# Latent attention in source order on four engines, key-tile maxima over two banks, block sums made by accumulating transfers

## The chip, the core and the metric

The kernel runs on one core of one Trainium2 chip. The metric is the time of one execution in microseconds (us). The engines are TensorE (PE, its weight loads listed apart as PEld), VectorE (DVE), ScalarE (ACT), GpSimd (POOL) and SyncE (SP), which only issues transfers here; 16 DMA engines move data between HBM and the core's memories, SBUF and PSUM. PSUM consists of banks of 512 32-bit values per partition.

## The reference

One encoder layer over 2304 tokens: a sequence of 2048 (the prompt) and one of 256 (the sample), which share weights but don't attend to each other. D_MODEL is 1024, all in 32-bit floats.

```python
h = rms_norm(x, g_mix_pre);  z = h @ w_in            # 1024 -> 256 + 128 + 32 + 3*512
c_q, c_kv, k_rope, nq, nk, nv = split(z)             # the first three are the "latents"
a = mla_attention(...)   # q = rms(c_q) @ w_q_up, k,v = rms(c_kv) @ w_kv_up, 8 heads,
                         # 96-wide keys, dense softmax(q k^T * scale) v, 64-wide values
n = neighborhood_attention(nq, nk, nv, na_rpb)       # 8 heads, window of 8 rows x 16 columns
x = x + rms_norm(concat([a, n]) @ w_o, g_mix_post)
h = rms_norm(x, g_ffn_pre)
hc = conv3(h @ w_ffn_up)                             # 1024 -> 5632, width-3 depthwise over tokens
g, u = split(hc)
x = x + rms_norm((gelu(g) * u) @ w_ffn_down, g_ffn_post)
```

## The kernel before

**Precision.** A factor is split into two rounded parts, "hi" and "lo": `split` (L93 to L96) is an ACT cast that writes hi (L95) and a DVE subtraction that writes lo (L96). A product of two split factors is three matmuls, hi·hi, lo·hi and hi·lo, which accumulate in one PSUM bank (`mm3`, L118 to L122).

**Stages in order**, with their stretch of the profile: input projection (0 to about 250 us), neighbourhood attention (250 to 695), preparation of the latent attention (695 to 793), latent attention (793 to 1657), output projection (1657 to 1910), FFN up (1910 to 2945), FFN down (2945 to 3497).

**Neighbourhood attention** runs 144 half-unit steps. Beside its own work a step carries a piece of other projections: up to step `mid` = 72 the queries and keys not yet projected (`queries_rest`), with weights in tiles `w2`; then the latent projection (`latents`, L480, 72 pieces, from step mid + 6 by `LATE`). At step mid the eight k-rows of the latents' weights are loaded and split in one burst through the `qk_hl` buffers.

**Latent attention** (`mla`, L539). For each head there are five units: four of 512 prompt queries against 16 key tiles of 128, one of 256 sample queries against 2 key tiles; 66 steps a head, 528 in all. A step's `scores` (L614) is three matmuls into `pS` (L619 to L621; three buffers), an exponential by ACT rounded to `ph` (L623), the same exponential unrounded in place (L624), DVE's difference `pl` (L626), and POOL's running sum `acc` (L634). Four steps later `values` (L638) adds two matmuls to the accumulators `po` and `pl` (L646, L647). At a unit's end `acc` is split and summed over keys, ACT and DVE take the accumulators out (`evacuate`, `add`) and `finish` (L670) transposes the result through a bank of `pm`, from which DVE takes a reciprocal and a quotient (L677, L679).

Each unit needs preparation while the one before it runs: `load` (L586) transposes its queries through `pm` and splits them from there, 16 `guard` tasks (L596; 2 for the sample) compute a hi·hi product of 128 queries with 512 keys into `pg` (L600) and its maximum (L602), and `peak` and `row` (L604, L608) turn the maxima into a row that is transposed through `pm` and appended to the queries, so that the exponential can't overflow. In heads 0 to 6 `k_chunk` (L561) also projects the next head's keys, 512 tokens at a time, three matmuls into `pm` (L120 to L122) and a split from there (`kbh`, `kbl`). `pm` has one buffer, shared by `load`, `row`, `k_chunk` and `finish`. `pg` has two.

The order of instructions on each engine in this stage comes from the framework's scheduler, which sorts by priorities and modelled durations; the source only says at which step a task is created (`spread`, `prepare`, L722 to L741). When the last head begins, `load_wo` (L898) loads and splits the eight 1024-wide rows of w_o one after the other.

**Output projection** (`out_proj`, L913): 18 token tiles, each transposed (L948), split, multiplied by w_o (48 matmuls), normed. In the first tiles `weight_sums` (L125) also loads blocks of w_ffn_up (48 loads), lets POOL form five sums or differences for six of the 22 column groups (L149) and stores them to the scratch `ws_d` in HBM. At tile 8 the FFN's pools open and its first loads start (`ffn_open`).

**FFN up** (`ffn`, L1183) is a Strassen-like scheme: for each of 3 token parts and 22 column groups j ("units", 66 of them) seven products m of 12 matmuls each (L1291), of a weight factor (a block of w_ffn_up or a sum of two blocks, `WRAW` and `WSUM`) and an x factor. In part 0, for j from 6 on, POOL forms the sums (`w_source`, L1122, five a unit, L1132) and stores them to `ws_d`; parts 1 and 2 load them. Each unit's products are combined with adds on DVE and POOL (L1194) from PSUM and from copies that ACT makes (L1231), then convolved, gated and stored.

Of the kernel before, what the change touches and what calls it, by code (L numbers as in the profile page):

```python
# [10 lines left out]
F32 = mybir.dt.float32  # L11
# [6 lines left out]
P = 128  # L18
# [28 lines left out]
class Layer:  # L47


    def __init__(self, ctx, tc, a):  # L50
# [17 lines left out]
        self.ws_d = scratch("ws_d", (NFF, 5, P, 512))  # L68
# [56 lines left out]
    def weight_sums(self, raw_buf, out_buf, todo):  # L125

        nc, a = self.nc, self.a
        raws, outs, stores = [], [], []
        todo = list(todo)

        def load():
            if todo:
                j, c = todo.pop(0)
                raw = [raw_buf().rearrange("p (a b) -> p a b", a=2) for _ in range(2)]
                for r in range(2):
                    for hf in range(2):
                        src = a["w_ffn_up"][j + r * NFF][:, 4 * hf + 2 * c:4 * hf + 2 * c + 2, :]
                        nc.sync.dma_start(out=raw[r][:, hf].rearrange("p (a b) -> p a b", b=P), in_=src)
                raws.append((j, c, raw))

        def sums():
            if outs:
                j, c, out = outs.pop(0)
                nc.sync.dma_start(out=self.ws_d[j].rearrange("n p k -> p n k")[:, :, c * 256:(c + 1) * 256], in_=out)
            if raws and (len(raws) > 1 or not todo):
                j, c, raw = raws.pop(0)
                out = out_buf().rearrange("p (n b) -> p n b", b=256)
                for m, ((r0, c0), (r1, c1), sign) in enumerate(self.WSUM.values()):
                    nc.gpsimd.tensor_tensor(out=out[:, m], in0=raw[r0][:, c0], in1=raw[r1][:, c1],  # L149
                                            op=ALU.add if sign > 0 else ALU.subtract)  # L150
                outs.append((j, c, out))

        def step():
            load()
            sums()

        def flush():
            while raws or outs:
                sums()

        return step, flush

    def front(self):
# [5 lines left out]
        with ExitStack() as s:  # L169
# [8 lines left out]

            def load_w(buf, W, c0, n, at=0):
                for k in range(KD):  # L180
                    raw = buf()
                    nc.sync.dma_start(out=raw[:, :n], in_=a["w_in"][k * P:(k + 1) * P, c0:c0 + n])
                    self.split(raw[:, :n], W[0][:, k, at:at + n], W[1][:, k, at:at + n])

            def qk_products(W, f, pq, ks, xh, xl):

                fc = slice(f * P, (f + 1) * P)
                for k in ks:
                    self.mm3(pq, W[0][:, k, fc], W[1][:, k, fc], xh[:, k, :], xl[:, k, :], k == 0, k == KD - 1)

# [37 lines left out]
            w2 = w_tiles(w2p, 3, 512)  # L228


            with ExitStack() as s1:
# [10 lines left out]
                W = [w_tiles(wp, i, n) for i, n in enumerate((512, 256, 256))]  # L242
                raw_buf = lambda: rawp.tile([P, 512], F32, name="raw")
# [35 lines left out]
                def queries(b, side):  # L279
                    xh, xl = blocks[b]  # L280
                    for f in range(4):
# [3 lines left out]
                        qk_products(W[1 + f // 2], f % 2, pq, range(KD), xh, xl)  # L285
# [9 lines left out]
                load_w(raw_buf, W[0], LAT + 1024, 512)  # L295
                n0[1]()
                load_w(raw_buf, W[1], LAT, 256)
# [3 lines left out]
                load_w(raw_buf, W[2], LAT + 512, 256)  # L301
                for b in range(nb):
# [6 lines left out]
                    if b in (2, 3):  # L309
                        load_w(raw_buf, w2, LAT + 512 * (b - 2) + 256, 256, 256 * (b - 2))  # L310
# [10 lines left out]
            sp = en(name="na_s", bufs=2)  # L321
            sm = en(name="na_sm", bufs=6)
# [145 lines left out]
            def queries_rest():  # L468
# [7 lines left out]
                qk_products(w2, f, Rest.pq, range(4 * half, 4 * half + 4), *Rest.blocks[b])  # L476
# [3 lines left out]
            def latents():  # L480
# [8 lines left out]
                for k in range(2 * part, 2 * part + 2):  # L489
                    self.mm3(Rest.pq, xh[:, k, off:off + P], xl[:, k, off:off + P], wlat[0][:, k, :], wlat[1][:, k, :],  # L490
                             k == 0, k == KD - 1)
# [4 lines left out]

            grids = [(0, 32, 4 * u) for u in range(8)] + [(SP, 4, 0)]
# [4 lines left out]
            LATE = 6  # L502
# [4 lines left out]
            for i in range(n + 6):  # L507
# [16 lines left out]
                if i + lead < mid:  # L524
                    queries_rest()
                if i == mid:
                    wlat = [w[:, :, :LAT] for w in w_tiles(w2p, 3, 512)]
                    Rest.n, Rest.blocks = 0, {0: fetch(0)}
                    load_w(lambda: st.tile([P, 2, NB], F32, name="qk_hl").rearrange("p a b -> p (a b)"), wlat, 0, LAT)
                if i >= mid + LATE and Rest.n < 4 * NT:  # L530
                    latents()
# [7 lines left out]
    def mla(self):  # L539
        nc, tc, a = self.nc, self.tc, self.a  # L540
        with ExitStack() as s:
# [15 lines left out]
            ps_g = en(name="ml_pg", bufs=2, space=PSUM)  # L557
# [11 lines left out]
            class Unit:  # L569


                def __init__(u, h, t0, nq, kt0, nkt):
                    u.h, u.t0, u.nq, u.kt0, u.nkt = h, t0, nq, kt0, nkt
                    u.nt = nq // P
                    u.nch = (nkt * P + 511) // 512
# [10 lines left out]
                def load(u):  # L586
# [7 lines left out]
                    u.mx = sm.tile([P, 4, 4], F32, name="mx")  # L594

                def guard(u, i, c):  # L596
                    n = min(512, u.nkt * P - c * 512)
                    pg = ps_g.tile([P, 512], F32, name="pg")
                    k0 = u.kt0 * P + c * 512
                    nc.tensor.matmul(out=pg[:, :n], lhsT=u.qh[0:QKD, i * P:(i + 1) * P],  # L600
# [884 lines left out]
```

## Time and profile before

| | us |
|---|---|
| median of 3 runs | 3509.79 (3509.08 to 3511.76) |
| the profiled execution | 3507.15 |
| its span | 3505.4 |
| PE busy in it | 3368.9 (96%) |
| DVE busy | 2385.9 (68%) |
| ACT busy | 1837.8 (52%) |
| POOL busy | 1376.2 (39%) |

The span is the traced part of the profiled execution; 1.75 us lie around it. A busy share says how full an engine was on average; where time is lost is read from stretches in which PE was not full, since PE carries most of the work in every stage. "PEclk" in the rows is the clock that TensorE was granted, as a share of full speed.

### The profile page before, as it was taken

Reading aid. Unit: us, or ns where it says so; the run is one execution under the profiler, and the core shown is the slowest. Engines: PE = TensorE matmul, PEld = TensorE weight load, DVE = VectorE, ACT = ScalarE, POOL = GpSimd, SP = SyncE. Lnnn points to the kernel's source line nnn. Section 1 sums busy time; section 2 is a strip of 40 time slices with the busy share of each in tenths; the row PEclk is TensorE's granted clock in tenths of the full one; section 3 lists DMA queues with packets and bytes.
Section 4 is the critical chain, followed back from the end, with each engine's and each line's share of the span. In section 5 each row is a group of like instructions: output and inputs, shape, how many; then the busy total and the mean of one; then the engine's idle time right before and its main releaser. Section 6 shows DMA issues by size and latency. Waiting matters only on the chain.

```text
span 3505.4 us, 51290 instructions
## 1 busy us (share of the span) xinstructions
PE 3368.9 (96%) x17806; PEld 2913.6 (83%) x17806; DVE 2385.9 (68%) x3774; ACT 1837.8 (52%) x3463; POOL 1376.2 (39%) x1216
## 2 busy tenths in 40 slices
PE   8999989989999999999989999899999999999999
PEld 7889979967777777766778999899989999888887
DVE  5325555588988888898345999987789776224332
ACT  4225556567777777777234544555555554223121
POOL 0022323157777778775521477632232222000110
PEclk9999999999999999999999999999999999999999
DMA  8789889341000000011995655465546555434553
GB/s 269 253 258 231 213 191 237 122 149 26 13 15 14 16 14 13 18 47 48 267 256 150 195 170 172 144 192 149 149 113 194 151 150 179 149 117 134 187 186 125
DMA packets 338068, 497.24 MB, mean 142 GB/s; under 512 B 69584, under 2 KB 213072, under 8 KB 330832
## 3 DMA queue, kind: packets, MB, share of 16 engines
q1 hardware_dynamic: 302576, 417.87, 39.7%
q0 software_dynamic: 35232, 76.10, 8.6%
q8 instruction: 140, 2.29, 0.3%
q14 instruction: 120, 0.98, 0.1%
HBM read 337.90 MB, written 155.37 MB: 141 GB/s over the span
## 4 chain that ended last, share of the span: by engine, by line
PE 74%; DVE 10%; ACT 6%; DMA 5%; issue 3%; POOL 2%; SPq 1%; ACTq 0%; POOLq 0%; DVEq 0%
PE pz L1291 21%; PE po L122 6%; PE po L120 6%; PE po L121 6%; PE po L646 3%; PE pS L619 3%; PE pg L600 3%; PE pl L647 3%; PE pS L621 3%; PE pS L620 3%; PE pO L448 2%; DVE wl L96 2%; PE pT L120 2%; PE pT L411 2%; PE pT L122 1%
## 5 line engine op out<-in xcount | busy, mean ns | idle before, releaser
L1291 PE MATMUL pz<-xh,wh 128*128 128x386 f32 (+1 forms) x1848 | 633.3, 343 | 20.8 <-DVE hg L1194 11.5
L1291 PE MATMUL pz<-xl,wh 128*128 128x386 f32 (+1 forms) x1848 | 630.2, 341 | 6.1 <-DVE xl L96 5.7
L1291 PE MATMUL pz<-xh,wl 128*128 128x386 f32 (+1 forms) x1848 | 628.8, 341 | 6.0 <-DVE wl L96 6.0
L634 POOL TENSOR_TENSOR acc<-acc,ph 128x512 f32<-128x512 f32 x434 | 568.3, 1309 | 103.8 <-ACT ph L623 82.3
L96 DVE TENSOR_TENSOR wl<-raw,wh 128x512 fp32r<-128x512 f32 (+1 forms) x470 | 444.0, 953 | 36.2 <-ACT wh L95 36.0
L95 ACT CAST wh<-raw 128x512 fp32r<-128x512 f32 (+1 forms) x470 | 288.9, 627 | 235.4 <-PE pz L1291 221.3
L623 ACT ACTIVATE ph<-pS 128x512 fp32r<-128x512 f32 (+1 forms) x528 | 312.4, 592 | 183.5 <-PE pS L621 98.6
L626 DVE TENSOR_TENSOR pl<-pS,ph 128x512 fp32r<-128x512 f32 (+1 forms) x528 | 354.6, 673 | 71.9 <-ACT pS L624 68.3
L110 POOL TENSOR_TENSOR rs_r<-rs_m,mhalf 128x1 f32<-128x1 f32 (+1 forms) x90 | 74.3, 826 | 800.4 <-DVE rs_m L107 800.1
L1291 PEld LDWEIGHTS pz<-xh,wh 128*128 128x128 f32 x1848 | 350.5, 190 | 31.3 <-DVE hg L1194 16.6
L1291 PEld LDWEIGHTS pz<-xl,wh 128*128 128x128 f32 x1848 | 351.1, 190 | 8.1 <-DVE xl L96 7.3
L1291 PEld LDWEIGHTS pz<-xh,wl 128*128 128x128 f32 x1848 | 350.7, 190 | 7.5 <-DVE wl L96 7.4
L602 DVE TENSOR_REDUCE mx<-pg 128x1 f32<-128x512 f32 (+1 forms) x528 | 343.0, 671 | 12.6 <-PE pg L600 10.1
L1241 POOL TENSOR_TENSOR cg<-cg,cu 128x768 f32<-128x768 f32 (+1 forms) x66 | 165.2, 2503 | 445.3 <-DVE cu L1225 324.6
L122 PE MATMUL po<-dh,xr 128*128 128x512 f32 x792 | 311.7, 394 | 0.4 <-DVE xr L96 0.4
L121 PE MATMUL po<-dl,xr 128*128 128x512 f32 x792 | 311.8, 394 | 0.0
L120 PE MATMUL po<-dh,xr 128*128 128x512 f32 x792 | 311.6, 393 | 0.0
L624 ACT ACTIVATE pS<-pS 128x512 f32<-128x512 f32 (+1 forms) x528 | 311.5, 590 | 0.0
L96 DVE TENSOR_TENSOR xr<-xt,xr 128x1408 fp32r<-128x1408 f32 x37 | 60.6, 1639 | 330.8 <-ACT xr L95 330.8
L95 ACT CAST xr<-xt 128x1408 fp32r<-128x1408 f32 x37 | 50.7, 1369 | 382.1 <-PE po L121 368.3
L619 PE MATMUL pS<-ql,kbh 96*128 96x512 f32 (+1 forms) x528 | 215.2, 408 | 5.0 <-DVE pl L626 2.9
L621 PE MATMUL pS<-qh,kbh 97*128 97x512 f32 (+1 forms) x528 | 211.8, 401 | 0.1
(259 smaller groups left out, 7923.6 us busy)
## 6 DMA issues: line engine op xcount, KB each, us to landing
raw<-ws_d SPq DMA_DIRECT2D x250, 256.0 KB, 2.7
raw<-in_w_ffn_up_dram SPq DMA_DIRECT2D x164, 256.0 KB, 3.2
xt<-g_d SPq DMA_DIRECT2D x37, 704.0 KB, 4.4
graw<-g_d SPq DMA_DIRECT2D x35, 704.0 KB, 5.1
g_d<-cg SPq DMA_DIRECT2D x110, 192.0 KB, 2.3
ws_d<-raw SPq DMA_DIRECT2D x80, 256.0 KB, 2.0
xl<-xs_d POOLq DMA_DIRECT2D x18, 1024.0 KB, 8.8
xh<-xs_d POOLq DMA_DIRECT2D x18, 1024.0 KB, 7.1
```

Source lines behind the costliest of these rows:

```text
L95: self.nc.scalar.copy(out=hi, in_=src)
L96: self.nc.vector.tensor_tensor(out=lo, in0=src, in1=hi.bitcast(F32), op=ALU.subtract)
L120: mm(out=out, lhsT=lh, rhs=rh, start=start, stop=False)
L121: mm(out=out, lhsT=lh, rhs=rl, start=False, stop=False)
L122: mm(out=out, lhsT=ll, rhs=rh, start=False, stop=stop)
L602: nc.vector.tensor_reduce(out=u.mx[:, i, c:c + 1], in_=pg[:, :n], axis=AX.X, op=ALU.max)
L619: mm(out=pS[:, :nq], lhsT=u.kh[0:QKD, kc], rhs=u.ql[:, :nq], start=True, stop=False)
L621: mm(out=pS[:, :nq], lhsT=u.kh[:, kc], rhs=u.qh[:, :nq], start=False, stop=True)
L623: nc.scalar.activation(out=ph[:, :nq], in_=pS[:, :nq], func=AF.Exp, scale=scale)
L626: nc.vector.tensor_tensor(out=pl[:, :nq], in0=pS[:, :nq], in1=ph[:, :nq].bitcast(F32), op=ALU.subtract)
L634: eng.tensor_tensor(out=u.acc[:, :nq], in1=ph[:, :nq].bitcast(F32), op=ALU.add, in0=u.p0[:, :nq].bitcast(F32) if j == 1 else u.acc[:, :nq])
L1291: nc.tensor.matmul(out=pz[:, :w], lhsT=l[:, kk, :], rhs=r[:, kk, :w], start=onto is None and kk == 0 and e == 0, stop=kk == 3 and e == 2, ...
```

## The change

It has six parts.

1. `weight_sums` now issues 16 HBM-to-HBM transfers on POOL's queue during the latent attention: 8 plain copies of blocks of w_ffn_up into `ws_d`, then 8 that add a second block, or an earlier sum, to them. Each covers 11 column groups (2.88 MB, 1408 runs of 2 KB). The loads, sums and stores in the output projection and `w_source` are gone. There are four sums, none with a minus, for all 22 groups.
2. The seven FFN products have other signs, so that the order within a unit is 1, 5, 3, 7, 2, 6, 4 and only product 4 accumulates onto another's bank (six banks a unit instead of five). `hu[0]` is formed by POOL, no longer by DVE; the value half comes before the gate half.
3. The latents' weights are loaded two steps apart through a pool of their own from step mid - 12 on and split one row per step into the tiles that the finished `w2` leaves; the latents begin at mid.
4. `pg` is one buffer of two banks: a guard task makes two products and one maximum over 1024. 264 maxima instead of 528.
5. In the latent attention the four engines PE, DVE, ACT and POOL keep the order of the source (`manual_schedule`). The tasks have new steps, and after a unit's last values no values are issued for two steps (`free`).
6. `load_wo` is spread: a load or a split at every third step or so of the last head.

The core of the diff:

```diff
+        for i, (m, (b0, b1)) in enumerate(self.WSUM.items()):
+            for js in (slice(0, 11), slice(11, NFF)):
+                first.append(lambda i=i, b0=b0, js=js: nc.gpsimd.dma_start(out=self.ws_d[js, i], in_=block(b0, js)))
+                src = self.ws_d[js, list(self.WSUM).index(b1)] if isinstance(b1, int) else block(b1, js)
+                stages[max(0, i - 1)].append(lambda i=i, src=src, js=js: nc.gpsimd.dma_start(
+                    out=self.ws_d[js, i], in_=src, accum_op=ALU.add, max_dma_last_dim=2048))
...
-            ps_g = en(name="ml_pg", bufs=2, space=PSUM)
+            ps_g = en(name="ml_pg", bufs=1, space=PSUM)
...
+                    n = min(1024, u.nkt * P - c * 1024)
+                    pg = ps_g.tile([P, 1024], F32, name="pg")
+                    k0 = u.kt0 * P + c * 1024
+                    for b in range(0, n, 512):
+                        e = min(n, b + 512)
+                        nc.tensor.matmul(out=pg[:, b:e], lhsT=u.qh[0:QKD, i * P:(i + 1) * P],
+                                         rhs=u.kh[0:QKD, k0 + b:k0 + e], start=True, stop=True)
                     nc.vector.tensor_reduce(out=u.mx[:, i, c:c + 1], in_=pg[:, :n], axis=AX.X, op=ALU.max)
...
+            LEAD = 5
+            for k, u in enumerate(order):
+                s0 = len(steps)
+                if k > 0:
+                    g0 = max(s0 - u.nkt - LEAD, 0)
+                    if k > 1:
+                        at(g0 - 10, u.fetch)
+                    at(g0 - 1, u.load)
+                    tasks = u.guards()
+                    for i, t in enumerate(tasks):
+                        at(g0 + i * (s0 - LEAD - g0) // len(tasks), t)
+                    at(s0 - LEAD, u.peak)
+                    at(s0 - LEAD + 2, u.row)
+                if k % 5 == 0 and u.h + 1 < H:
+                    for i, c0 in zip((4, 12, 20, 28, 38), range(0, ST, 512)):
+                        at(s0 + i, lambda h=u.h + 1, c0=c0: k_chunk(h, c0))
+                steps += [(u, j) for j in range(u.nkt)]
+            for q, part in enumerate(self.weight_sums()):
+                for r, f in enumerate(part):
+                    later.setdefault((20, 160, 270, 360)[q] + 8 * r, []).append(f)
...
-                        self.load_wo()
+                        for r, f in enumerate(self.load_wo()):
+                            later.setdefault(i + 6 + 3 * r + r % 2, []).append(f)
...
-                        later.setdefault(i + 1.5, []).append(u.evacuate)
-                        later.setdefault(i + 2, []).append(u.add)
+                        free = i + 2
+                        later.setdefault(i + 1, []).extend([u.evacuate, u.add])
                         later.setdefault(i + 9, []).append(u.finish)
...
-            if t < 7:
-                sums()
-                sums()
-            if t == 7:
-                flush()
...
-        self.w_source(i + 2)
...
-                tt(nc.gpsimd, u.v[:, :w], u.s[4][:, :w], u.s[5][:, :w], -1)
+                tt(nc.gpsimd, u.v[:, :w], u.s[1][:, :w], u.s[5][:, :w], -1)
             if m == 2:
+                u.t = hp.tile([P, 388], F32, name="t")
+                tt(nc.vector, u.t[:, :w], u.v[:, :w], u.b[2][:, :w], -1)
                 u.hu = hp.tile([P, 2, 388], F32, name="hu")
-                tt(nc.vector, u.hu[:, 0, :w], u.b[2][:, :w], u.s[4][:, :w], 1)
-                u.t = hp.tile([P, 388], F32, name="t")
-                tt(nc.vector, u.t[:, :w], u.s[1][:, :w], u.b[2][:, :w], -1)
+                tt(nc.gpsimd, u.hu[:, 0, :w], u.s[7][:, :w], u.t[:, :w], -1)
```

PE's order in the latent attention, before: where a unit is finished (`pm<-ident,s`), in the middle of another unit. `pS` are scores, `po` and `pl` values, `pg` guards.

```order
L619 MATMUL pS<-ql,kbh_7801 128x512
L620 MATMUL pS<-qh,kbl_7802 128x512
L621 MATMUL pS<-qh,kbh_7801 128x512
L600 MATMUL pg<-kbh_7801,qh 128x512
L647 MATMUL pl<-pl,vt_7800 65x512
L646 MATMUL po<-ph,vt_7800 128x512 x2
L674 MATMUL pm<-ident,s 128x65 x4
L619 MATMUL pS<-ql,kbh_7801 128x512
L620 MATMUL pS<-qh,kbl_7802 128x512
L621 MATMUL pS<-qh,kbh_7801 128x512
L647 MATMUL pl<-pl,vt_7800 65x512
```

The same engine afterwards, at step 12 of a head (lines are two or fewer further on in that file): `finish`, then a chunk of the next head's keys (`pm<-ch,wkh` and so on), then a unit's queries (`pm<-ident,qs`).

```order
L620 MATMUL pS<-ql,kbh_7849 128x512
L621 MATMUL pS<-qh,kbl_7850 128x512
L622 MATMUL pS<-qh,kbh_7849 128x512
L647 MATMUL po<-ph,vt_7848 128x512
L648 MATMUL pl<-pl,vt_7848 65x512
L675 MATMUL pm<-ident,s 128x65 x4
L120 MATMUL pm<-ch,wkh 64x512
L121 MATMUL pm<-cl,wkh 64x512
L122 MATMUL pm<-ch,wkl 64x512
L588 MATMUL pm<-ident,qs 96x128 x4
L620 MATMUL pS<-ql,kbh_7849 128x512
```

Three users of the one `pm` buffer now follow one another with no scores or values between them.

POOL's order in part 0 of FFN up, before: `raw` are the sums of weight blocks, `cg` the gate's product, `v` a combination of two copies.

```order
L1132 TENSOR_TENSOR raw<-raw 128x512 x5
L1241 TENSOR_TENSOR cg<-cg,cu 128x2x384
L1194 TENSOR_TENSOR v<-s_22916,s_22874 128x386
L1132 TENSOR_TENSOR raw<-raw 128x512 x5
L1241 TENSOR_TENSOR cg<-cg,cu 128x2x384
L1194 TENSOR_TENSOR v<-s_23084,s_23042 128x386
```

Afterwards, in the same place:

```order
L1158 TENSOR_TENSOR v<-s_21929,s_21950 128x386
L1205 TENSOR_TENSOR cg<-cg,cu 128x2x384
L1158 TENSOR_TENSOR hu<-s_21994,t 128x386
L1158 TENSOR_TENSOR v<-s_22089,s_22110 128x386
L1205 TENSOR_TENSOR cg<-cg,cu 128x2x384
L1158 TENSOR_TENSOR hu<-s_22154,t 128x386
```

The five sums of a unit are gone, and one combination (`hu`) has come to POOL.

## Rows read from the trace of the kernel before

**Rows 1.** Windows: length, busy (count) of PE, PEld, DVE, ACT, POOL; clock, DMA, GB/s
```profile
470.00:520.00 50.00, 36.05 (x217) 32.74 (x216) 27.12 (x65) 27.74 (x68) 15.36 (x22) 0.83 0.93 208
690.00:710.00 20.00, 13.20 (x67) 11.42 (x66) 8.31 (x19) 8.19 (x25) 9.62 (x20) 0.83 0.46 131
793.00:1657.00 864.00, 843.84 (x3748) 603.24 (x3746) 770.81 (x1338) 668.84 (x1297) 661.29 (x515) 1.00 0.08 20
1540.00:1600.00 60.00, 53.65 (x215) 35.22 (x214) 54.89 (x85) 44.72 (x80) 41.64 (x31) 0.97 0.24 76
1670.00:1820.00 150.00, 133.30 (x633) 109.36 (x632) 66.09 (x91) 44.51 (x70) 65.12 (x85) 0.95 0.94 269
...
1925.00:2265.00 340.00, 326.13 (x1796) 316.01 (x1795) 338.43 (x346) 167.07 (x276) 221.47 (x124) 1.00 0.57 177
2265.00:2300.00 35.00, 24.04 (x105) 22.53 (x104) 34.00 (x31) 19.72 (x26) 15.52 (x6) 0.80 0.50 163
2300.00:2595.00 295.00, 295.00 (x1667) 295.00 (x1666) 227.28 (x325) 163.15 (x262) 66.92 (x40) 1.00 0.55 155
2595.00:2645.00 50.00, 42.53 (x219) 41.09 (x217) 49.50 (x45) 30.63 (x42) 21.65 (x7) 0.93 0.33 100
```

**Rows 2.** Waits, 460 to 530 us: engine line, waited for: total us, times, longest
```profile
ACT w3h L95 <- DMA qk_hl<-in_w_in_dram: 15.4, 4, 9.6
...
PE pT L411 <- ACT pb L404: 10.0, 1, 10.0
```

**Rows 3.** One latent step in time: start us, us, engine, line, operation, out<-in
```profile
1003.65 0.59 ACT L623 ACTIVATE ph<-pS 128x512 fp32r<-128x512 f32 x1
...
1003.91 0.40 PE L621 MATMUL pS<-qh,kbh 97*128 97x512 f32 x1
...
1004.13 0.60 ACT L624 ACTIVATE pS<-pS 128x512 f32<-128x512 f32 x1
...
1004.38 0.39 PE L647 MATMUL pl<-pl,vt 128*65 128x512 f32 x1
```

**Rows 4.** DVE's groups, 800 to 1530 us: xcount | busy us, mean ns | idle before
```profile
L626 DVE TENSOR_TENSOR pl<-pS,ph 128x512 fp32r<-128x512 f32 (+1 forms) x449 | 301.3, 673 | 62.3 <-ACT pS L624 59.1
...
L96 DVE TENSOR_TENSOR al<-acc,ah 128x512 fp32r<-128x512 f32 (+1 forms) x34 | 31.5, 928 | 0.7
...
L96 DVE TENSOR_TENSOR kbl<-pm,kbh 64x512 fp32r<-64x512 f32 (+1 forms) x34 | 21.0, 618 | 0.0
...
L679 DVE TENSOR_TENSOR ot<-pm,rd 128x256 f32<-128x256 f32 (+1 forms) x33 | 12.7, 385 | 0.0
L677 DVE RECIPROCAL rd<-pm 128x4 f32<-128x4 f32 (+1 forms) x33 | 5.7, 171 | 5.8 <-PE pm L674 5.8
```

**Rows 5.** Waits of PE, 800 to 1530 us
```profile
PE pm L674 <- DVE ot L679: 2.0, 7, 0.3
```

**Rows 6.** The guards' maxima: ns min/median/max, first and last start, forms
```profile
L602 DVE TENSOR_REDUCE mx<-pg x528: 410/679/694, 747.4 to 1626.2; 128x1 f32<-128x512 f32 x168, 128x1 f32<-128x256 f32 x8
```

**Rows 7.** Issues on POOL: ns min/median/max, first and last start
```profile
L225 POOL DMA_DIRECT2D v<-nav_d x24: 759/878/1117, 107.1 to 614.3; - x24
```

**Rows 8.** POOL's DMA queue in the whole span: packets, MB, share of 16 engines
```profile
q0 software_dynamic: 35232, 76.10, 8.6%
```

**Rows 9.** Waits, 1670 to 1820 us
```profile
PE pt L948 <- DMA at<-att_d: 15.5, 4, 7.1
```

**Rows 10.** The chain of waits, around 1794 us: start us, us, what
```profile
1793.88 10.86 DMA at<-att_d
```

**Rows 11.** Groups, 1925 to 2265 us (FFN up, part 0)
```profile
L96 DVE TENSOR_TENSOR wl<-raw,wh 128x512 fp32r<-128x512 f32 x150 | 183.3, 1236 | 0.0
L1132 POOL TENSOR_TENSOR raw<-raw 128x512 f32<-128x512 f32 x80 | 135.4, 1692 | 72.5 <-DVE wl L96 66.1 <-DMA raw<-in_w_ffn_up_dram 4.0
```

**Rows 12.** Groups, 2300 to 2595 us (FFN up, part 1)
```profile
L96 DVE TENSOR_TENSOR wl<-raw,wh 128x512 fp32r<-128x512 f32 x142 | 107.7, 761 | 18.4 <-ACT wh L95 18.4
...
L1194 POOL TENSOR_TENSOR v<-s,s 128x386 f32<-128x386 f32 x20 | 22.3, 1114 | 37.1 <-ACT s L1231 35.0 <-DMA g_d<-cg 2.1
```

More of the change, by code (lines that the diff above doesn't have):

```diff
@@ L122, in mm3, with weight_sums @@
         mm(out=out, lhsT=ll, rhs=rh, start=False, stop=stop)
-    def weight_sums(self, raw_buf, out_buf, todo):
+    def weight_sums(self):
         nc, a = self.nc, self.a
[L128 to L154, printed above, removed]
-            sums()
-        def flush():
-            while raws or outs:
-                sums()
-        return step, flush
+        block = lambda rc, js: a["w_ffn_up"].rearrange("(r j) p k c -> r j p (k c)", r=2)[
+            rc[0], js, :, 512 * rc[1]:512 * rc[1] + 512]
+        first, stages = [], [[], [], []]
+        for i, (m, (b0, b1)) in enumerate(self.WSUM.items()):
[4 more added lines that the diff above has]
+                    out=self.ws_d[js, i], in_=src, accum_op=ALU.add, max_dma_last_dim=2048))
+        return [first] + stages
     def front(self):
@@ L227, in front @@
             hps = [hp0]
-            w2 = w_tiles(w2p, 3, 512)
+            w2 = [[w2p.tile([P, KD, P], F32R, name=f"w{2 * f + i}") for i in range(2)] for f in range(4)]
             with ExitStack() as s1:
@@ L321, in front @@
             sp = en(name="na_s", bufs=2)
+            lwp = en(name="na_lw", bufs=2)
             sm = en(name="na_sm", bufs=6)
@@ L525, in front @@
                     queries_rest()
+                if 0 <= i - (mid - 10) < KD:
+                    lat_w[i - (mid - 10)]()
+                if 0 <= i - (mid - 12) < KD:
+                    lat_w[i - (mid - 12)] = load_lat(i - (mid - 12))
+                if i == mid - 4:
+                    Rest.blocks = {0: fetch(0)}
                 if i == mid:
[L527 to L530, printed above, removed]
+                    Rest.n = 0
+                if i >= mid and Rest.n < 4 * NT:
                     latents()
@@ L761, in mla @@
                     t()
+                for t in side.pop(i, []):
+                    t()
                 if i < len(steps):
-                    u, j, side = steps[i]
+                    u, j = steps[i]
                     if u.h == H - 1 and early is not None:
@@ L770, in mla @@
                         later.setdefault(i + 2.5, []).append(u.high_sums)
-                    for t in side:
-                        t()
                 for t in later.pop(i + 0.5, []):
@@ L775, in mla @@
                 n = 0
-                while flight and n < 2 and (len(flight) > 4 or i >= len(steps)):
+                while flight and n < 2 and i >= free and (len(flight) > 4 or i >= len(steps)):
                     u, j, ps = flight.pop(0)
```

188 lines of the change are left out of this document (69 added, 119 removed).

## The prediction

> **What bounds the kernel now.** I read the window table first [rows 1]. PE is what a stage waits for: it is full in 2300 to 2595 us (295.00 of 295), and where it isn't, its clock falls as well (.83 in 470 to 520, .80 in 2265 to 2300). So I look for stretches in which PE has gaps, and then in the waits for what ends last there. Four places matter. In the neighbourhood attention PE has 36.05 busy us of 50 around step mid; one wait of 10.0 us for ACT stands there, and ACT itself waits for the burst of latent weights (15.4 us, longest 9.6) [rows 2]. In the output projection PE has 133.30 of 150 at a DMA share of .94 [rows 1] and waits 15.5 us for `at` [rows 9]. In part 0 of FFN up DVE is busy for 338.43 of 340 us [rows 1]. In the latent attention the table has PE at 843.84 of 864, but matmuls overlap there: one lasts .39 to .40 us, and from L621 to L647, two products later, pass .47 us [rows 3], so the next can start every .235 us. A head has 404 long products (4 units of 16 steps x 5, 64 guards, 12 key products, 8 for the sums), 94.9 us; 17 of half the length and 54 short transposes add some 6.5 (an estimate by their columns). That is 101.4 a head, some 803 us for eight (811 less 8, since the last has no keys to prepare). The stage takes 861 us from its first exponential to the last values, so PE loses 58, seven a head, and more where w_o is split: 53.65 of 60 in 1540 to 1600 [rows 1].
>
> **Latent weights, spread.** The burst goes. Lost there: 14 us of idle time and 8.5 by the clock (50 x .17) [rows 1]. The eight splits are still ACT's and DVE's work, but one a step, loaded two steps ahead. The latents, which start six steps sooner, no longer fill the tail (13.20 of 20 busy in 690 to 710). I take -17; bounds -10 (the wait alone [rows 2]) and -22 (all of it).
>
> **Output projection.** 60 transfers and 60 POOL sums go, about a third of what moves at .94 share. Idle 16.7 and clock 7.5 (150 x .05) make 24 [rows 1]. One event of 10.86 us [rows 10] comes from the FFN's own first loads, which stay. I take -13; bounds -8 and -20.
>
> **FFN up.** 80 POOL sums of 1692 ns [rows 11] and 80 stores go. DVE's subtraction `wl` takes 1236 ns beside them and 761 in part 1 [rows 11, 12]: 150 x .475 = 71 us of DVE's time. PE did 1796 products in 340 us; at part 1's 1667 in 295 these need 318, so 22 are lost, and 35 - 105/5.65 = 16 in the stretch that follows, where DVE is busy for 34.00 of 35 [rows 1]. The latter, like the 11 lost in 2595 to 2645, hangs on the x factors of the next part, which the change leaves; a third of it may go, with the backlog. First-unit losses of about 4 stay. That is -25. Against it, `hu[0]` comes to POOL, 66 times at about 1.11 us (the row of `v`, the same form) [rows 12], and contends with DVE. Beside POOL's sums a split of 1236 against 761 ns shows what that costs.
>
> The Trainium skill says the same (SBUF — State Buffer, Who interferes with whom): a DVE instruction with two SBUF inputs and a GpSimd instruction that reads SBUF exclude one another for their whole length. By that rule all of POOL's 66 x 1.11 = 73 us would be lost to DVE; the trace agrees with the direction, and since DVE has 295 - 227 = 68 us to spare in 20 units [rows 1], the sum would hardly move by it.
>
> I charge 3 for it, because PE runs ahead of DVE there: -22, bounds -28 and -10. FFN down keeps its instructions: 0. The preparation loses or gains a microsecond with the paired maxima: +1.
>
> **Latent attention, the `pm` buffer.** This decides the sign. In the old order the scheduler kept `finish`, `k_chunk`, `load` and `row` apart: PE waited for `pm` seven times, longest .3 us [rows 5]. In the new order of PE, as the block of the section on the change shows, `finish`, `k_chunk` and `load` stand back to back at steps 12 and 28 of a head. Count from the start X of the step's last score product. The scores are there at X + .40; ACT's pair takes 1.08 (1003.65 to 1004.73) [rows 3], DVE's subtraction .67 [rows 4], and DVE, in source order, does that first: X + 2.15. PE is at `finish` at X + .70 (three products), through it at about X + 1.0; reciprocal .17 and quotient .385 [rows 4] free the bank at X + 2.7. PE stands for 1.7, with the next step's scores queued behind it. Then three products, a cast by ACT (at most the .60 of an exponential [rows 3]) and `kbl` .62 [rows 4]: 1.4 more until `load` may begin. With hand-overs 3.3, twice a head. `finish` then `load` at step 44: 1.9. The four rows a head come one step behind a load or two behind a finish: .3 and .65, twice each. Together 6.6 + 1.9 + 1.9 = 10.4 us a head in heads 1 to 6, 8.6 in the first, 5 in the last: 76, taken as 75. Bounds: 2 (only what the rows show now) and 95.
>
> **Guards.** A maximum of 256 columns takes 410 ns, one of 512 679 [rows 6]; a line through both gives 1.22 us for 1024 (bounds .68, no dearer, and 1.36, double). With one buffer of two banks the next pair's products wait until that maximum is done. The loop is two products .64, up to .67 of subtraction ahead of it on DVE, 1.22, and some .35 of hand-overs (an estimate): 2.9 us, against 12 products x .235 = 2.82 that PE has in two steps. So .1 x 18 windows x 8 heads = 14; bounds 0 and 36.
>
> **The rest of that stage.** Unit ends (`al` .93 [rows 4], held values): 12 (8 to 24). Load and split of w_o, spread over 48 steps: 8 in place of about 12, bounds 4 and 14. Clock after new stalls, as in 1540 to 1600 at .97 or worse: 10, bounds 0 and 27. So 803 + 75 + 14 + 12 + 8 + 10 = 922 against 861: **+61**. Not all ends meet: bounds +28 and +95.
>
> **Transfers on POOL.** Issuing costs 759 to 1117 ns for 512 to 1024 runs [rows 7]; carried on to 1408 runs about 1.4 us, 16 times, while `acc` can fall behind by a few steps: 0. The queue moved 76.10 MB for 8.6% of 16 engines x 3505 us [rows 8]: 63 engine-us a MB, so 2.88 MB take 11.4 us on 16 engines; an adding one isn't shown, from the same to three times that. The stages lie over 90 steps (some 145 us) apart, and the DMA share is .08 [rows 1]. The bound on the other side: if an issue keeps POOL for the whole transfer, 16 x 8 = 130 us beyond what the buffers of `ph` hide.
>
> The Trainium skill (DMA: Bandwidth & Descriptors, Why a DMA increments its semaphore by 16 and not by 1) says that a transfer runs on the largest number of engines up to 16 that divides its slowest dimension. By that these, with 11 groups, would use 11 engines and take 16.6 us, an estimate; the sum stays the same. No row here shows a transfer of this shape.
>
> **Sum.** 3507.15 - 17 - 13 - 22 + 61 + 1 = 3517 for a profiled execution. The median of the runs is 2.6 above the profiled one: 3520, and I say **3521** (rounding up for POOL's issues).
>
> **Rivals.**
> *Faster.* PE does not stand at `pm`, because by steps 12 and 28 it runs behind ACT and DVE and the bank is free when it comes. For it: the waits of .3 now [rows 5], and DVE's idle time, 62.3 us before `pl` [rows 4]. Against it: `kbl` and `load` follow in the same step, and their work cannot begin before the products that PE has just made. The stage is then 922 - 75 = 847, -14, and the kernel 3521 - 75 = **3446**. Half of the stall gives 3483.
> *Cancelled.* A `pm` stall of some 55 to 67 us instead of 75, no other change: **3510**.
> *Much slower.* POOL is held by its transfers: `acc` stops, the exponentials run out of `ph` buffers, and PE stands about 8 us sixteen times: 3521 + 130 = **3650**; with the adding ones alone, 3586. It decides once an issue lasts longer than about six steps, 9 us. Against it: an issue of 1024 runs is over in 1.1 us [rows 7].
>
> **Chances.** My forecast (slower by the `pm` queue, 3517 to 3565) .44; faster .34; cancelled .15; held POOL .07. A difference of .2%, 7 us, is about what a measurement can tell from none. The three gains outside the stage have rows behind them (-52 in all, -28 to -70), so the sign hangs on the price of `pm`, which no row shows. Thus faster .34, same .15, slower .51. The likeliest case alone runs from 3517 to 3565 by the bounds of its terms; the range reaches to the middle of the faster rival and to the lesser one of held transfers: 3445 to 3578.
>
> **What would show it.** Right: in the profile after, PE's waits in the latent stage name `pm`, with over 40 us on the lines of the chunk's first product, the queries' transposes and the row, and a head takes 114 us or more. Wrong: these waits stay under 10 us. The maxima show 1.2 us each, and PE's wait for them under .2. POOL's issues are 1 to 2 us, with no gap in `acc`. The 10 us wait near step mid is gone. `wl` in part 0 is near 760 ns and DVE under 80% busy there. The forecast falls if a head takes less than 109 us, or if the gains outside the stage are under 30.

## The result, and the profile after

The changed kernel takes 3598.34 us (median of 4 runs, 3592.32 to 3602.05) against 3510.78 us (4 runs) of the kernel before on the same chip: a ratio of 1.0246, 95% interval 1.0228 to 1.0263. It is slower by 88 us; some 10 had been forecast, and the time lies 20 us above the range. The profiled execution's span is 3596.7 us, 91 more than before.

By stage, from the first and last starts of the stages' own instructions (before, after, in us; the forecast as a change):

| | before | after | forecast |
|---|---|---|---|
| first exponential of the latent attention | 794.0 | 786.9 | -16 |
| latent attention, first to last exponential | 859.3 | 977.8 | +61 |
| from there to FFN up's first product | 257.1 | 256.3 | -13 |
| FFN up, first to last product | 1034.7 | 1013.2 | -22 |

The windows of the profile after that answer to [rows 1] (length, busy us and count of PE, PEld, DVE, ACT, POOL; clock, DMA share, GB/s):

```profile
470.00:520.00 50.00, 46.79 (x310) 43.63 (x309) 30.29 (x72) 30.41 (x74) 17.53 (x27) 0.97 0.98 237
690.00:710.00 20.00, 8.69 (x36) 7.09 (x37) 9.53 (x33) 11.19 (x39) 11.83 (x30) 0.66 0.47 132
785.00:1764.00 979.00, 869.69 (x3743) 624.79 (x3743) 758.38 (x1078) 679.49 (x1290) 676.79 (x528) 0.95 0.27 64
...
1764.00:1792.00 28.00, 13.99 (x46) 9.37 (x45) 8.32 (x20) 5.26 (x10) 3.11 (x5) 0.67 0.64 163
1792.00:1812.00 20.00, 20.00 (x89) 16.43 (x88) 8.06 (x13) 3.87 (x7) 1.76 (x4) 0.95 0.46 151
2035.00:2375.00 340.00, 331.89 (x1862) 330.10 (x1861) 286.46 (x343) 192.51 (x296) 120.07 (x68) 0.99 0.52 156
2410.00:2705.00 295.00, 291.43 (x1629) 291.11 (x1630) 238.75 (x295) 164.56 (x256) 102.38 (x61) 0.99 0.50 149
```

Around step mid PE now has 46.79 busy us of 50, and in part 0 of FFN up 1862 products where it had 1796. The latent stage has as many products as before (3743 recorded, 3748 before) in 979 us, at a granted clock of .95 instead of 1.00. A new hole stands at 1764 to 1792, where the output projection begins: 13.99 busy us of 28 at a clock of .67; the 28 us after the latent stage had 24.84 before (1652 to 1680).

What PE waits for in the latent stage (790 to 1700 us: total, times, longest), where there had been 2.0 us at `pm` in all [rows 5]:

```profile
PE pm L120 <- DVE ot L680: 24.8, 13, 2.0
PE pg L601 <- DVE mx L603: 24.7, 41, 1.7
PE pm L588 <- DVE kbl L96: 19.4, 14, 1.4
PE pm L588 <- issue: 15.9, 8, 2.9
PE pm L612 <- DVE ot L680: 11.5, 14, 0.8
PE po L647 <- DVE o L668: 1.7, 7, 0.3
```

The four rows with `pm` add up to 71.6 us: the queue of the forecast (75). "issue" at L588 is the queries' load behind a finish, eight times about 2 us. One of the steps with three users, in PE's order of time (start, us):

```profile
1050.10 0.40 PE L621 MATMUL pS<-qh,kbl 96*128 96x512 f32 x1
1050.33 0.40 PE L622 MATMUL pS<-qh,kbh 97*128 97x512 f32 x1
1050.56 0.40 PE L647 MATMUL po<-ph,vt 128*128 128x512 f32 x1
1050.80 0.39 PE L648 MATMUL pl<-pl,vt 128*65 128x512 f32 x1
1051.03 0.41 PE L675 MATMUL pm<-ident,s 65*128 65x65 f32 x4
1053.33 0.55 PE L120 MATMUL pm<-ch,wkh 128*64 128x512 f32 x1 [1.89 <-DVE ot L680]
1053.67 0.63 PE L121 MATMUL pm<-cl,wkh 128*64 128x512 f32 x1
1054.10 0.63 PE L122 MATMUL pm<-ch,wkl 128*64 128x512 f32 x1
1056.12 1.09 PE L588 MATMUL pm<-ident,qs 128*96 128x128 f32 x4 [1.39 <-DVE kbl L96]
...
1057.86 0.63 PE L622 MATMUL pS<-qh,kbh 97*128 97x512 f32 x1
1058.28 0.63 PE L647 MATMUL po<-ph,vt 128*128 128x512 f32 x1
...
1060.60 0.39 PE L620 MATMUL pS<-ql,kbh 96*128 96x512 f32 x1
```

X is 1050.33, and the bank is free at 1053.3, X + 3.0 (2.7 in the forecast). But the products do not then start every .235 us: from 1053.67 to about 1060.5 they start every .43 us and last .63, at a granted clock of .50, the lower of its two levels, 1.2 GHz. They are slow from the first stall on, before the second. The bracketed idle times, 3.3 us, are joined by some 2 us of slower work: from the queries' transposes at 1056.12 to the score product at 1060.60 pass 4.48 us, and 2.94 for the same instructions in experiment 5, where the clock stays up.

### The profile page after: what moved, and what is told of

The parts are those of the page before. It is cut to its first block, busy times and chain, and to the rows that moved or that the text cites. A ratio compares the mean times of both kernels' runs of the same rounds, so it can differ in the third digit from the quotient of the medians.

```text
span 3596.7 us, 50824 instructions
## 1 busy us (share of the span) xinstructions
PE 3383.3 (94%) x17806; PEld 2934.2 (82%) x17806; DVE 2317.6 (64%) x3468; ACT 1864.1 (52%) x3479; POOL 1296.8 (36%) x1158
## 4 chain that ended last, share of the span: by engine, by line
PE 73%; DVE 9%; ACT 6%; DMA 4%; issue 3%; POOL 2%; SPq 0%; ACTq 0%; POOLq 0%; DVEq 0%
PE pz L1255 24%; PE po L120 7%; PE po L122 7%; PE po L121 7%; PE pg L601 3%; PE pS L622 2%; PE pS L620 2%; PE pS L621 2%; PE pO L431 2%; PE po L647 2%; PE pl L648 2%; ACT ph L624 2%; DVE mx L603 2%; PE pT L120 2%; DVE pl L627 2%
## 5 line engine op out<-in xcount | busy, mean ns | idle before, releaser
L603 DVE TENSOR_REDUCE mx<-pg 128x1 f32<-128x1024 f32 (+1 forms) x272 | 317.9, 1169 | 18.6 <-PE pg L601 18.3
L96 DVE TENSOR_TENSOR xr<-xt,xr 128x1408 fp32r<-128x1408 f32 x37 | 61.8, 1670 | 333.1 <-ACT xr L95 333.1
L1158 POOL TENSOR_TENSOR v<-s,s 128x386 f32<-128x386 f32 (+1 forms) x66 | 103.8, 1572 | 432.0 <-DVE cg L1189 285.9
L647 PE MATMUL po<-ph,vt 128*128 128x512 f32 (+1 forms) x528 | 211.6, 402 | 3.3 <-DVE o L668 3.3
```

What stands on the lines that cost most here:

```text
L96: self.nc.vector.tensor_tensor(out=lo, in0=src, in1=hi.bitcast(F32), op=ALU.subtract)
L603: nc.vector.tensor_reduce(out=u.mx[:, i, c:c + 1], in_=pg[:, :n], axis=AX.X, op=ALU.max)
```

## The experiments

Each run is compared with runs of the kernel before on its own chip (medians of 3503 to 3511 us there); below are ratios, and the length of the latent stage from its first to its last exponential (859.3 us before, 977.8 after).

**1. Two chunks moved** (`e1_chunk`).

```diff
-                    for i, c0 in zip((4, 12, 20, 28, 38), range(0, ST, 512)):
+                    for i, c0 in zip((4, 10, 20, 26, 38), range(0, ST, 512)):
```

> Two of the five key chunks of a head are moved from steps 12 and 28 to steps 10 and 26, so that three users of the pm bank no longer follow one another in one step; finish and load still do, at 12, 28 and 44. Theory (the clock falls only after two waits close together): the wait between chunk and load goes, 14 x 1.65 = 23 us, and with it the half clock that follows the double stalls, some 25 us: about 3550 us. Rival (a single wait of 2 us costs the clock as well): only the 23 us, about 3575 us. If the clock is no part of it at all, the granted clock of the latent stage stays at .95.

3563.82 us, ratio 1.0163 (1.0145 to 1.0182); the stage took 946.1 us, 32 less, at a clock of .97. The time lies between the two figures. The waits for `pm` fell only from 71.6 to 57.5 us, since PE now waits for 22 loads behind a finish (43.3 us) and no longer for eight; the rest of the 32 us goes with the clock. The theory's "only after two waits" falls, for single waits are followed by half clock too:

```profile
1035.22 0.92 PE L588 MATMUL pm<-ident,qs 128*96 128x128 f32 x4 [1.84 <-issue]
...
1036.79 0.63 PE L622 MATMUL pS<-qh,kbh 97*128 97x512 f32 x1
```

**2. All users of `pm` apart** (`e2_apart`).

```diff
-                    at(g0 - 1, u.load)
+                    at(g0 - (3 if u.nkt == 2 else 1), u.load)
...
-                    at(s0 - LEAD + 2, u.row)
+                    at(s0 - LEAD + 3, u.row)
...
-                    for i, c0 in zip((4, 12, 20, 28, 38), range(0, ST, 512)):
+                    for i, c0 in zip((4, 16, 20, 34, 38), range(0, ST, 512)):
...
-                        later.setdefault(i + 9, []).append(u.finish)
+                        later.setdefault(i + 5, []).append(u.finish)
```

> All users of the pm bank are kept at least two steps apart (finish 5 instead of 9 steps after the last values, chunks at 4, 16, 20, 34, 38, the row one step later, the sample's load two steps earlier). Theory (the pm queue with its clock is most of the loss): PE's waits for pm fall from 72 us to under 10, the stage loses some 95 us: about 3503 us. Rival (the single guard buffer takes their place, since DVE loses the time in which it caught up): PE's waits for the maxima rise from 25 us to 60 or more, about 3545 us.

3489.17 us, ratio 0.9947 (0.9929 to 0.9966): below the kernel before. The theory holds and the rival falls. The stage's window, and what is left of PE's waits there (no row with `pm` above 2.0):

```profile
780.00:1654.00 874.00, 843.84 (x3745) 613.55 (x3744) 751.46 (x1078) 678.70 (x1291) 677.85 (x528) 0.98 0.30 72
```
```profile
PE pg L601 <- DVE mx L603: 23.7, 35, 1.7
```

The stage became 105 us shorter (977.8 to 872.6) by an edit of step numbers alone: the 72 us of waits, and 33 more. The granted clock accounts for about as much: it withheld 979 x .05 = 49 us after the change and withholds 874 x .02 = 17 here. The clock isn't back at 1.00, because the single waits for the maxima remain; behind this one PE runs at half clock until 1161:

```profile
1150.90 0.28 PE L601 MATMUL pg<-kbh,qh 96*128 96x256 f32 x1
1152.89 0.72 PE L601 MATMUL pg<-kbh,qh 96*128 96x512 f32 x2 [1.72 <-DVE mx L603]
...
1155.32 0.63 PE L620 MATMUL pS<-ql,kbh 96*128 96x512 f32 x1
...
1161.62 0.40 PE L621 MATMUL pS<-qh,kbl 96*128 96x512 f32 x1
```

**3. Guards as before, in source order** (`e3_g512`): two buffers of 512, 528 maxima.

```diff
-            ps_g = en(name="ml_pg", bufs=1, space=PSUM)
+            ps_g = en(name="ml_pg", bufs=2, space=PSUM)
...
-                    u.nch = (nkt * P + 1023) // 1024
+                    u.nch = (nkt * P + 511) // 512
```

> The guards are as before the change: two buffers of 512, 16 tasks with one product and one maximum each; the source order stays. Theory (the one guard buffer costs what PE's waits for the maxima show, 25 us, and some of the clock): 3565 to 3573 us. Forecast on record: 14 us, 3584 us. Rival (the 264 more maxima cost DVE 1.36 instead of 1.22 us a pair, and every later subtraction comes later): 3598 us or more.

3570.05 us, ratio 1.0173 (1.0157 to 1.0189); stage 952.7. The paired guards cost 25 to 28 us here, twice the forecast. One maximum was sized rightly (the trace has 272 of them, not 264):

```profile
L603 DVE TENSOR_REDUCE mx<-pg x272: 406/1215/1227, 741.9 to 1731.7; 128x1 f32<-128x1024 f32 x120, 128x1 f32<-128x256 f32 x16
```

The forecast's average loop missed the unevenness: where the sample's guard and the next unit's first pair stand in one step, the whole loop is open.

```profile
1078.85 0.28 PE L601 MATMUL pg<-kbh,qh 96*128 96x256 f32 x1
1080.84 0.51 PE L601 MATMUL pg<-kbh,qh 96*128 96x512 f32 x1 [1.70 <-DVE mx L603]
```

**4. Both** (`e7_apart_g512`), the edits of 2 and 3.

> The users of pm kept apart, as in the run with them two steps apart (3489 us), and the guards as before the change (two buffers of 512). Theory (the waits for the one guard buffer are a loss of their own, 28 us in the run with that alone): about 3461 us. Rival (with pm apart the maxima are hidden and the doubled number of reductions weighs): 3480 us or more.

3457.13 us, ratio 0.9853 (0.9838 to 0.9869); stage 838.8 us, 34 less than in 2, and the clock is back:

```profile
772.00:1614.00 842.00, 820.51 (x3745) 610.29 (x3746) 771.23 (x1328) 679.26 (x1291) 678.55 (x528) 1.00 0.31 75
```

The guards' cost is one of its own and even larger without the `pm` queue: 24 us of waits in 2, and the clock that fell behind them. With both repaired the stage in source order is 20 us shorter than the 859.3 of the scheduler's order before the change.

**5. Filled stalls** (`e13_fill`, again as `e13_fill_b` beside the unaltered changed kernel, `e15_after`). PE works through the stalls, and what it waits for comes no sooner: from the finish to the chunk pass 2.3 us in both.

```diff
+            def fill(n):
+                u, j = current[0]
+                if 0 < j < u.nkt - 2 and u.nkt == 16:
+                    for _ in range(n):
+                        nc.tensor.matmul(out=u.pl[0:HD + 1, :], lhsT=self.zero, rhs=rhs, start=False, stop=False)
```

> The changed kernel with useless products of a zero factor (they add nothing to an accumulator) set into the stalls for pm: 7 between finish and the chunk, 6 between the chunk and the load, 7 between finish and load at step 44, some 210 in all, 49 us of PE work of .2335 us each, none longer than the stall it fills. The waits for pm stay as long as they were. Theory (a part of the loss is TensorE's half clock after the double stalls): the stretches at half clock in the latent stage go, 23 to 30 us less, 3568 to 3575 us, though PE has more to do. Rival (the clock is no cost of its own): 3598 us, or 10 more for the hand-overs.

> The filled stalls again (some 210 useless products of a zero factor in the waits for pm). Theory (the half clock after double stalls is a cost of its own): 15 to 20 us under the unaltered changed kernel. Rival (the first difference lay between chips): within 5 us of it.

First 3581.56 us, ratio 1.0222 (1.0201 to 1.0243), some 8 us below the changed kernel by the ratios, with intervals that overlap; then, on one chip, 3576.28 against 3600.07 us, ratios 1.0190 (1.0172 to 1.0209) and 1.0250 (1.0234 to 1.0265), which do not. PE did some 50 us more work and the kernel was 24 us faster there. The same place in the second of these runs, with the stage's window:

```profile
1043.36 1.81 PE L735 MATMUL pl<-vt,zero 128*65 128x512 f32 x7
1045.44 0.41 PE L122 MATMUL pm<-ch,wkh 128*64 128x512 f32 x1 [0.27 <-DVE ot L682]
...
1046.16 1.54 PE L735 MATMUL pl<-vt,zero 128*65 128x512 f32 x6
1047.71 0.64 PE L590 MATMUL pm<-ident,qs 128*96 128x128 f32 x4
...
1050.65 0.39 PE L622 MATMUL pS<-ql,kbh 96*128 96x512 f32 x1
```
```profile
784.00:1744.00 960.00, 895.11 (x3962) 634.05 (x3960) 760.43 (x1083) 681.39 (x1295) 677.54 (x528) 0.99 0.28 65
```

The chunk still starts 2.1 us after the fill began, but products then last .41 us instead of .55 to .63, and the stage's clock is .99 instead of .95. So TensorE's clock is a cost of its own, of the gaps and not of the work: some 24 us in the comparison on one chip, 8 in the first.

**6. Zero columns early** (`e5_zc`, `e5_zc_b`). Three small transfers, `x_d<-zc`, had been issued at 795 us; after the change SyncE issues them at the head of the output projection, and its queue stands for 6.55 us before the first `na` (start, us):

```profile
1772.95 0.38 SPq L682 DMA_DIRECT2D att_d<-ot  x1
...
1775.91 6.55 SPq L932 DMA_DIRECT2D x_d<-zc  x3
1782.50 0.67 SPq L939 DMA_DIRECT2D na<-natt_d  x1
```

```diff
+            for c0, n in ((0, 1), (SP + 1, 2), (XC - 1, 1)):
+                nc.sync.dma_start(out=self.x2_d[:, :, c0:c0 + n], in_=self.zc[:, :, :n])
             i = free = 0
             ordered = ExitStack()
```

> The zero columns of the FFN's input are written to memory before the latent attention instead of at the start of the output projection, where their transfers held the queue of SyncE for 6.6 us ahead of the first loads. Theory (this holds up the output projection's first tiles): 7 to 10 us less, 3588 to 3591 us. Rival (the hole there is the last unit's own chain, which nothing overlaps now): 3598 us.

> The zero columns written before the latent attention, again. Theory (they held SyncE's queue at the start of the output projection): 6 to 10 us under the unaltered changed kernel. Rival (nothing but chance in the stage's length): within 3 us of it.

The first time 3596.51 us, ratio 1.0251 (1.0235 to 1.0266): no difference, with a stage of 990.1 us in its profile that hid the rest. On one chip with the unaltered kernel: 3589.84 against 3600.07 us (ratio 1.0224, 1.0204 to 1.0244; the intervals touch). From the last exponential to FFN up's first product passed 249.9 us against 256.3. So 6 to 10 us, part of the hole. By the order of events in the profile the rest is the last unit's chain of sums, quotient, store and load, and products at half clock behind it (.67 in the 28 us); no run takes these apart.

**7. Order released 16 steps early** (`e8_release`, on top of 2).

> The users of pm kept apart (3489 us), and the source order ends 16 steps before the latent attention does, so that the scheduler may lay the output projection's first tiles beside the last unit. Theory (the hole at the start of the output projection comes from the order being fixed to the last instruction): 8 to 16 us less, 3473 to 3481 us. Rival (the hole is the first transfers' lateness): 3489 us.

3493.17 us, ratio 0.9959 (0.9944 to 0.9974), as 2, and 257.2 us from the last exponential to FFN up (255.6 in 2): fixing these last 16 steps is not what makes the hole.

**8. Scheduler's order again** (`e4_sched`: no `manual_schedule`; `e6_mlabefore`: the latent attention as before the change).

> The changed kernel with the same tasks at the same steps, but the order on the four engines is left to the framework's scheduler, as before the change. Theory (the loss comes from the order in which three users of pm follow one another, which the scheduler undoes): PE's waits for pm under 10 us, the latent stage near 875 us, the output projection starts without its hole: 3480 to 3495 us. Rival (the paired guards, the spread of the tasks or the transfers on POOL cost the stage its time under any order): over 3530 us.

> The latent attention and the split of w_o as before the change (scheduler's order, 528 guards, two buffers of 512); the transfers of block sums stay at the same steps, and so do the changes in the neighbourhood attention, the output projection and the FFN. Theory (those parts gain what their stages showed or would show without the hole: 8 + 13 + 21): 3465 to 3472 us. Rival (the transfers on POOL slow the stage, or the output projection gains nothing in itself): 3482 us or more.

3674.27 and 3664.60 us, ratios 1.0474 (1.0459 to 1.0490) and 1.0443 (1.0425 to 1.0460): on the rivals' side, and far beyond, for a reason that neither named. The latent stage itself was as the theories had it, 873.7 and 858.4 us, but it began at 965.5 and 977.5 us. The first transfers on POOL in `e4_sched` tell why (ns, first and last start), with the window of the neighbourhood attention:

```profile
L135 POOL DMA_DIRECT2D ws_d<-in_w_ffn_up_dram x8: 1116/1142/1324, 1.4 to 285.4; - x8
```
```profile
250.00:700.00 450.00, 389.23 (x2718) 365.25 (x2718) 197.56 (x460) 190.41 (x450) 107.97 (x153) 0.92 0.98 232
```

They depend on nothing, so the scheduler put them first, and PE did 2718 products where it did 3139 in the 440 us from 250 (DMA share .98 against .85). In the changed kernel the order of POOL keeps them at 825.9 us and later, where the DMA engines had been nearly idle (.08 in [rows 1]). One reason of the second rival holds: from the last exponential to FFN up pass 254.8 us in `e6_mlabefore`, so the output projection gains only 2 there.

**9. POOL alone in source order** (`e11_pool`; `e12_mlabefore_pool` with the old latent attention).

> The changed kernel, but only POOL keeps the order of the source in the latent attention; TensorE, VectorE and ScalarE are left to the scheduler. Theory (without an order on POOL the 16 transfers went to the kernel's first 600 to 880 us, where the DMA engines are full, and delayed the latent stage's start from 785 to 962 us; the stage itself took 877): the start is back near 780 and the total 3490 to 3500 us. Rival (the scheduler's placement delays the early stages by other means): over 3600 us.

> The latent attention as before the change, in the scheduler's order on three engines, with POOL alone in source order so that the transfers stay in that stage. Theory (the stage takes 863 us as before, the FFN gains 20, the neighbourhood attention 8, the output projection nothing): 3480 to 3486 us. Rival (POOL's fixed order or the transfers slow the stage): 3500 us or more.

3622.29 and 3564.35 us, ratios 1.0335 (1.0312 to 1.0358) and 1.0171 (1.0151 to 1.0191). The starts are back, at 781.6 and 778.6 us, as the theory said, but the stages take 1004.9 and 946.5 us; both theories fall in the total, and the rival of the second stands. In `e12_mlabefore_pool`, counted by every 66th exponential, heads 3 and 6, which carry no transfer, take 108.9 and 107.9 us, and heads 0 to 2, 4 and 5, which do, 116 to 129. In the changed kernel heads 1 to 6, with and without transfers, take 122.7 to 123.1, and in `e2_apart` 108.6 to 110.4, so in the source order of all four engines the transfers cost nothing that shows. That the scheduler places the other engines' work by a longer duration of a transfer than its 1.1 to 1.9 us is argued, not shown.

**10. The neighbourhood attention as before** (`e14_na`, beside `e15_after`).

> The changed kernel once more, unaltered, beside the three that follow, so that differences of 10 to 20 us are read within one chip. Both theories: 1.0246 of the kernel before, about 3595 us.

> The changed kernel with the input projection and the neighbourhood attention as before the change: the latents' weights come in one burst at step mid again. Theory (the starts of the latent attention in the profiles so far, 772 to 786 us against 789, say that the spread weights gain some 10 us): 7 to 12 us above the unaltered changed kernel. Forecast on record: 17 us above. Rival (only the place of the loss moves): within 3 us.

3606.67 us, ratio 1.0269 (1.0253 to 1.0284), 6.6 above the unaltered one, with intervals that overlap; the latent attention starts 9.3 us later (789.0 against 779.7). The spread weights gain some 7 to 9 us, not 17.

**11. Together** (`e10_best`: 2, 3 and 6).

> The version with the pm users apart and the old guards (3457 us), and the zero columns written before the latent attention. Theory (the output projection's stage was 7.5 us shorter in the run with that alone, whose total hid it): 3450 us. Rival (the stage's gain there was chance): 3457 us.

3442.17 us, ratio 0.9822 (0.9803 to 0.9841): faster than both kernels. Its latent stage, and the 28 us behind it, which were 13.99 busy us after the change:

```profile
782.00:1623.00 841.00, 821.45 (x3743) 610.96 (x3743) 770.22 (x1328) 679.31 (x1290) 679.45 (x528) 0.99 0.31 75
```
```profile
1623.00:1651.00 28.00, 18.46 (x74) 13.03 (x73) 10.47 (x24) 5.96 (x11) 3.10 (x4) 0.82 0.70 222
```

## Why the prediction was wrong

The sign and the `pm` queue were right, the size was not: a profiled execution of 3517 was forecast and 3598 came. Of the 81 us, 57 lie in the latent attention (+61 forecast, some +118 measured), 9 ahead of it, 12 in the output projection and some 2 behind FFN up. What failed first is the sum for the latent stage, 922 us against 978: its clock term, 10, came out at some 33 (what no wait names), the guards, 14, at up to 34, and the rest, 20, at 36. Besides, two gains outside the stage came out below their lower bounds. By the table those gains are 29 us in all, and under 30 the forecast was to fall by its own words. The range ends at 3578, below the rival at 3586 that it is said to reach.

- **The `pm` queue** (75): 71.6 us of waits at the places that were named, and heads of 123 us (114 or more had been asked for). Right.
- **"Clock after new stalls: 10, bounds 0 and 27"**: this term failed. The clock was .95 over 979 us, 49 us by the forecast's own way of pricing it. Taking the gaps at `pm` away gave back 33 us beyond their waits; filling them gave back 24 on one chip. The forecast took the clock from a stretch whose share costs 60 x .03 = 2 us, and no row of before had stalls at `pm` behind which the price could be read.
- **Guards** (14): 25 to 34 us. The maximum, 1.215 us against 1.22, was right; an average loop of .1 us a window was not, since PE's waits are 41, up to 1.7 us, where "under .2" had been expected, and the clock falls behind some of them.
- **The rest of the stage** (20): with both repaired the stage is 838.8 us at a clock of 1.00, 36 above the floor of 803. Unit ends and the split of w_o were priced too low together; the runs do not divide them.
- **Latent weights** (-17): the wait at step mid is gone and PE gains 10.7 busy us there, but the tail that the latents filled stays empty (8.69 busy of 20 in 690 to 710) and the preparation that follows runs no faster. Worth 7 to 9, under the bound of 10.
- **Output projection** (-13): the loads and sums did go, and PE is full from 1792 to 1812 (20.00 of 20), but a hole opened before, and the stretch gained 0.8 us. The forecast's gain was there to be had: with the zero columns early it takes 246.6 us in `e10_best`, 10.5 less than before. The forecast named no first wait of the changed stage. Why the zero columns moved from 795 to 1775 us is open: it happens in the scheduler's order too.
- **FFN up** (-22): -21.5. The number was met in part by luck: counted by its 1848 products a part, part 0 gained 12.6 us (22 forecast), and parts 1 and 2 gained 4.4 and 4.5. The reason was only half right: `wl` still takes 958 ns there, and DVE is busy for 286 of 340 us (84%, not under 80). The five sums are gone, but `hu` came, and POOL's own adds are dearer:

```profile
L96 DVE TENSOR_TENSOR wl<-raw,wh 128x512 fp32r<-128x512 f32 x155 | 147.6, 958 | 2.6 <-ACT wh L95 1.0
...
L1158 POOL TENSOR_TENSOR v<-s,s 128x386 f32<-128x386 f32 x22 | 34.7, 1578 | 141.9 <-DVE cg L1189 110.1 <-ACT s L1195 11.1 <-DVE hg L1158 8.7
L1158 POOL TENSOR_TENSOR hu<-s,t 128x386 f32<-128x386 f32 x22 | 31.1, 1412 | 59.6 <-DVE t L1158 59.6
```

  In part 1 `v` had taken 1114 ns [rows 12] and takes 1477 now, and `wl` 938 instead of 761. Part 1 became no longer by it, so DVE's spare time covered it, as the forecast had said.
- **Transfers on POOL** (0, and the rival of a held POOL): an issue takes 1.08 us, an adding one 1.91, and heads with them are as long as heads without. The rival of a held POOL did not come.

```profile
L135 POOL DMA_DIRECT2D ws_d<-in_w_ffn_up_dram x8: 1079/1079/1163, 825.9 to 928.0; - x8
...
L137 POOL DMA_DIRECT2D ws_d<-in_w_ffn_up_dram x4: 1892/1910/1952, 1088.0 to 1134.9; - x4
```

The misses have one direction: a wait was priced by its own length, and a gain by the loss that it removes. The clock behind a wait was left to the bounds, and the next wait behind a gain was not priced.

## What to carry to other kernels

When an order is written by hand, list for every single-buffered bank who uses it in which step; three users in one step cost each the whole latency of the engines between them, and moving step numbers by one to six gave back 105 us here. Price a gap in TensorE's work with the slow stretch behind it, and look at a step's worst place, not at the mean. The transfers that depend on nothing went to the program's start under the scheduler, so what is meant to fill an idle stretch must be tied to it.

## What the runs showed of the hardware

- Stalls of under 2 us can be followed by products at half clock, and need not be. One of 1.89 us was, from 1053.67 to about 1060.5, with a second stall of 1.39 us in between; so were single ones of 1.84 us (`e1_chunk`) and 1.72 us (`e2_apart`). One of 1.95 us, later in the same head as the first, was not:

```profile
1119.89 0.62 PE L588 MATMUL pm<-ident,qs 128*96 128x128 f32 x4 [1.95 <-issue]
...
1120.58 0.40 PE L621 MATMUL pS<-qh,kbl 96*128 96x512 f32 x1
```

  What tells them apart no run here shows.
- Useless products in the gaps brought the granted clock of the stage from .95 to .99 and made the kernel 24 us faster on one chip.
- An adding transfer of the same 2.88 MB costs POOL 1.91 us to issue against 1.08 for a copy, and lands after 24.7 to 44.6 us against 13.5 to 15.9. The forecast's estimate with 16 engines had been 11.4 us. By the Trainium skill (DMA: Bandwidth & Descriptors, Why a DMA increments its semaphore by 16 and not by 1) such a transfer uses 11 engines, and 16.6 us were worked out from that, an estimate. The copies' times, issue and latency included, lie between the two, and no row shows how many engines took part. The times to landing, copies first:

```profile
DMA to landing us min/median/max: 13.5/14.2/15.9
...
DMA to landing us min/median/max: 24.7/29.9/44.6
```
